# A hybrid decoder layer in five fronts: one, two, two, two and one block instead of four pairs

## The chip, the cores and the metric

The kernel runs on one core of a Trainium2 chip. The metric is device time in microseconds (us) of one execution: the median of 3 runs was 4762.22 us before the change (4757.62 to 4777.23).

## What is computed

One decoder layer for 1024 prompt tokens and 8 sample tokens, everything in fp32, D = 1024:

```python
h = RMSNorm(x)
x = x + W_out(sigmoid(gate_ssd) * SSD(h) + sigmoid(gate_rwkv) * RWKV7(h))   # one projection of h, 7952 columns
x = x + MemCrossAttn(RMSNorm(x), mem_k, mem_v)                              # 4 heads, 256 memory tokens
x = x + PEER(RMSNorm(x))                                                    # per token 8 heads x 16 experts
y = RMSNorm(x)
```

SSD and RWKV-7 carry a state from token to token, so blocks of tokens go in order. PEER chooses 128 experts a token out of 16384 (two score vectors of 128 a head, their 16 best each, the 16 best of the sums), and computes `sum_k gate_k * gelu(x . U[i_k]) * V[i_k]` with the rows of two tables of 64 MB each.

## The kernel before

The 1024 prompt tokens are 8 blocks of 128, numbered 0 to 7. `front(gi)` (L464) takes a group of blocks (`GROUPS`, L20: four pairs) through everything up to the choice of experts: the **mixer** (norm, all columns of `w_in` in 31 weight tiles of 1024 x 256, each loaded in two halves of 512 KB; convolution, SSD; the RWKV inputs, a 31-step inverse of triangular 32 x 32 blocks at L843; the gates), then `scan(b)` a block, two chunks each, then `rest` (L1036): `w_out`, `w_mq`, attention over the memory, `w_mo`, `w_pq`, scores and the choice (`Best.add`, `Best.pairs`, tiles `q3b`). Products are `by_channel` (a 128 x 128 weight piece is stationary, the tokens move) or `by_token` (the tokens are stationary, 256 weight columns move).

Front 0 computes its mixer with split numbers: `parts` (L282) writes each weight tile as a rounded fp32r part and the rest (a ScalarE copy, a VectorE subtraction at L292, 1024 columns each), `Parts` does the same with the tokens, and `three` (L295) makes three products of a pair. It uses seven row buffers (tag `U`) and `xa` buffers for that. Its `rest` runs one block at a time (`SPLIT`). `memory()` (keys and values of the memory, through two `xa` buffers and `U` rows) and `keys()` are written behind front 0's scans, `sample_recurrences` behind front 0. Fronts 1 and 2 carry the 8 sample tokens along.

Experts work on one block and one of its 128 choices at a time. `u_step` gathers a row of U for each token (an indirect DMA that POOL issues, 512 KB, into a `U` row buffer) and multiplies it with x on VectorE (L1518). `v_step` (L1554) gathers a row of V and adds it, times its coefficient, on VectorE (L1570); for the k in `slots` TensorE adds it through a diagonal matrix (tile `dg`, PSUM tile `pv`). Beside front 1 stand the U and V steps of blocks 0 and 1, beside front 2 U of 2 and 3 and V of 2, beside front 3 U of 4 and 5 (`GATHERED`, L38); behind these V of block 3 (VectorE) and of block 4 (half of its steps on TensorE, `LATE_SLOTS`). The fronts' buffers are then closed, and in their space lie a 128 KB a partition matrix `cmat` and new rows. U of block 6 follows, and then V of blocks 5 and 6 by a **dense sum** (L1625): `spread` (L1591) writes each token's coefficients into `cmat` (128 tokens x 16384), and all of V passes in 128 blocks of 128 rows (`Vx`) through TensorE. One block in three multiplies plain fp32, the others split numbers. Between the dense blocks stand U and V of block 7, with 48 V steps on TensorE (`TAIL_SLOTS`, L34).

What is ready on an engine, and not yet held back by a buffer, is put in order when the program is built: program order is the priority, and a planner interleaves the engines' queues by its own costs. In program order front gi stands ahead of the expert steps of the group before it. Buffers of one tag go round in program order. Weights are loaded by the SyncE queue, gathers by POOL's.

## Time and profile before

| | before |
|---|---|
| median of 3 runs | 4762.22 us |
| profiled execution | 4803.32 us (span of its instructions 4801.6) |
| granted TensorE clock, mean | 0.800 |
| bytes moved by DMA | 1369.20 MB, mean 285 GB/s |

Busy tenths in 40 slices of 120 us (9 is 90% or more; PEclk is the granted TensorE clock in tenths; DMA the mean busy share of the 16 DMA engines):

```profile
PE   7889865769887786687676953588867964089995
DVE  4662296998878779988786899877773798786775
PEclk9988887889856896888668976688578985589997
DMA  4342589899978997999799897999788888889997
```

How to read the rows below. A row of a window table reads: stretch in us from the span's start, its length, then for each engine its busy time and its instructions (all: PE matmul, PEld weight load, DVE = VectorE, ACT = ScalarE, POOL = GpSimd; filtered by a line or a tile: only the engines that work on it), then the granted TensorE clock, the busy share of the DMA engines, and GB/s. A row of a line or form reads: line, engine, operation, out<-in with buffer numbers left out, partitions x elements, count | busy us, mean ns of one | idle us before it and what ended it. A row of a tile reads: shortest/median/longest in ns, first to last start in us. L114 is the helper `mm`, L120 the helper `copy`, L256 `weights`, L1514 `gather`.

### The profile page before, as it was taken

The page shows a single profiled execution, that of the slowest core. Times are in us where ns is not written, and L with a number is a line of the kernel's source. Part 1 is how long each engine was busy: PE and PEld are TensorE (multiplying, and loading weights), DVE is VectorE, ACT ScalarE, POOL GpSimd, SP SyncE. Part 2 cuts the span into 40 slices and gives each one's busy share as a digit, 9 for nine tenths or more (in the row PEclk, how much of TensorE's full clock was granted, in tenths as well). Part 3 has the DMA queues.
Part 4 walks back from the last instruction along what each step waited for, and adds up shares of the span by engine and source line. Part 5 has one row for each costly group of instructions (what it writes and reads, how often), then busy time and mean ns, then how long its engine had stood idle before and what let it go on. Part 6 is the DMA issues. An engine that isn't in the chain of part 4 may idle for free.

```text
span 4801.6 us, 56531 instructions
## 1 busy us (share of the span) xinstructions
PE 3581.8 (75%) x18486; PEld 2721.1 (57%) x18486; DVE 3656.8 (76%) x7730; ACT 1345.3 (28%) x3461; POOL 2456.4 (51%) x2059
## 2 busy tenths in 40 slices
PE   7889865769887786687676953588867964089995
PEld 6778764557565674365555742465655623056663
DVE  4662296998878779988786899877773798786775
ACT  5544322123132221232232311231321222143331
POOL 0000044765657644655566567745563566754444
PEclk9988887889856896888668976688578985589997
DMA  4342589899978997999799897999788888889997
GB/s 121 99 140 62 195 285 324 269 319 347 342 256 301 360 345 255 343 331 340 269 312 337 318 322 246 335 296 331 224 314 284 283 290 272 309 285 364 354 363 266
DMA packets 609102, 1369.20 MB, mean 285 GB/s; under 512 B 86124, under 2 KB 332296, under 8 KB 608800
## 3 DMA queue, kind: packets, MB, share of 16 engines
q0 software_dynamic: 260352, 948.03, 55.8%
q1 hardware_dynamic: 348456, 417.57, 26.2%
q8 instruction: 146, 2.39, 0.2%
q14 instruction: 148, 1.21, 0.1%
HBM read 1335.60 MB, written 29.90 MB: 284 GB/s over the span
## 4 chain that ended last, share of the span: by engine, by line
PE 40%; DVE 29%; DMA 11%; issue 10%; ACT 5%; POOL 4%; SPq 1%; another core or an unknown queue 0%; POOLq 0%; DVEq 0%; ACTq 0%
PE pp L114 21%; PE pc L114 10%; DVE U L1518 8%; DVE acc L1570 4%; PE pv L114 4%; POOL U L1514 4%; DMA U<-in_expert_u_dram,idx 3%; DMA U<-in_expert_v_dram,idx 2%; PE pg L114 2%; DVE q3b L452 2%; DVE vs L1618 1%; PE tp L114 1%; DMA w<-in_w_in_dram 1%; DVE f L581 1%; DVE q3b L455 1%
## 5 line engine op out<-in xcount | busy, mean ns | idle before, releaser
L1514 POOL DMA_INDIRECT U<-in_expert_u_dram,idx x1024 | 1280.9, 1251 | 828.9 <-DVE act L1518 249.4
L1518 DVE CUSTOM_DVE_ANT_0 U<-U,xa 128x1024 f32<-128x1024 f32 x1032 | 1271.1, 1239 | 140.8 <-DMA U<-in_expert_u_dram,idx 132.8
L1514 POOL DMA_INDIRECT U<-in_expert_v_dram,idx x768 | 900.7, 1173 | 751.4 <-DVE act L1518 248.0
L1570 DVE SCALAR_TENSOR_TENSOR acc<-U,cf,acc 128x1024 f32<-128x1024 f32 x656 | 863.5, 1316 | 111.4 <-DMA U<-in_expert_v_dram,idx 102.5
L114 PE MATMUL pp<-qw,w 128*128 128x256 f32 (+2 forms) x2872 | 731.3, 407 | 159.6 <-issue 43.8
L114 PEld LDWEIGHTS pp<-qw,w 128*128 128x128 f32 x2872 | 580.6, 214 | 281.8 <-issue 107.3
L114 PE MATMUL pp<-w,qw 128*128 128x256 f32 (+1 forms) x2528 | 623.0, 400 | 116.8 <-ACT f L856 44.5
L114 PEld LDWEIGHTS pp<-w,qw 128*128 128x128 f32 (+1 forms) x2528 | 477.4, 192 | 242.7 <-ACT f L856 46.9
L114 PE MATMUL pv<-U,dg 128*128 128x512 f32 x448 | 240.8, 669 | 99.1 <-DMA U<-in_expert_v_dram,idx 85.6
L114 PEld LDWEIGHTS pv<-U,dg 128*128 128x128 f32 x448 | 88.8, 209 | 217.5 <-issue 147.6
L114 PE MATMUL pc<-vs,cs 128*128 128x512 f32 x510 | 204.3, 455 | 1.9 <-DVE vs L1648 1.9
L114 PE MATMUL pp<-q,w 128*128 128x128 f32 (+1 forms) x1024 | 187.2, 340 | 4.5 <-DMA w<-in_w_pq_dram 3.3
L123 POOL TENSOR_TENSOR q3b<-q3b,q3b 128x400 f32<-128x400 f32 (+1 forms) x130 | 152.1, 1184 | 55.8 <-DVE q3b L452 53.2
L114 PEld LDWEIGHTS pp<-q,w 128*128 128x128 f32 x1024 | 163.3, 202 | 19.1 <-issue 3.7
L114 PE MATMUL pp<-vs,cs 128*128 128x512 f32 x510 | 172.2, 392 | 0.0
L114 PE MATMUL pc<-rst,q 64*64 64x64 f32 x1024 | 170.5, 305 | 2.2 <-issue 1.2
L114 PE MATMUL pg<-q,q 64*128 64x128 f32 (+1 forms) x384 | 110.8, 447 | 71.6 <-DMA q<-kt_d 33.3
L306 PE MATMUL tp<-ident,g 128*128 128x128 f32 (+1 forms) x296 | 60.8, 340 | 138.0 <-DVE g L1020 50.5
L114 PE MATMUL pc<-g,q 128*64 128x64 f32 x1024 | 140.0, 317 | 23.1 <-issue 16.6
L1648 DVE TENSOR_TENSOR vs<-Vx,vs 128x512 fp32r<-128x512 f32 x170 | 111.7, 688 | 42.1 <-ACT vs L120 35.0
L114 PEld LDWEIGHTS pg<-q,q 64*128 64x128 f32 (+1 forms) x384 | 82.5, 276 | 94.1 <-ACT q L1130 40.1
L306 PEld LDWEIGHTS tp<-ident,g 128*128 128x128 f32 (+1 forms) x296 | 43.2, 179 | 157.7 <-issue 56.2
(506 smaller groups left out, 6336.3 us busy)
## 6 DMA issues: line engine op xcount, KB each, us to landing
w<-in_w_in_dram SPq DMA_DIRECT2D x248, 512.0 KB
Vx<-in_expert_v_dram SPq DMA_DIRECT2D x128, 512.0 KB
w<-in_w_pq_dram SPq DMA_DIRECT2D x80, 512.0 KB
w<-in_w_out_dram SPq DMA_DIRECT2D x40, 512.0 KB
w<-in_w_mq_dram SPq DMA_DIRECT2D x40, 512.0 KB
w<-in_w_mo_dram SPq DMA_DIRECT2D x40, 512.0 KB
U<-in_expert_u_dram,idx POOLq DMA_INDIRECT x1024
U<-in_expert_v_dram,idx POOLq DMA_INDIRECT x768
```

The lines of the kernel that those rows point to most:

```text
L114: T.matmul(out, a, b, start=first, stop=last)
L123: G.tensor_tensor(out, a, b, op=op)
L306: T.transpose(p[:, j * P:j * P + n], x[:, c * P:(c + 1) * P], ident[:n, :n])
L452: V.tensor_tensor(oh[:n], iota50[:n, None, :].to_broadcast([n, 8, NCAND]), posf[:n, h, k8].unsqueeze(2).to_broadcast([n, 8, NCAND]), op=OP ...
L455: V.tensor_reduce(idf[:n, h, k8], oh[:n], axis=AX.X, op=OP.add)
L581: V.scalar_tensor_tensor(acc[:, 3 - k:TP], p[:, :TP - 3 + k], cw(k), acc[:, 3 - k:TP], op0=OP.mult, op1=OP.add)
L1514: G.indirect_dma_start(out=dst, out_offset=None, in_=table, in_offset=bass.IndirectOffsetOnAxis(ap=idx, axis=0))
L1518: V.tensor_tensor_reduce(out=u, in0=u, in1=x, scale=1.0, scalar=0.0, op0=OP.mult, op1=OP.add, accum_out=out)
L1570: V.scalar_tensor_tensor(z["acc"], v, cf, z["acc"], op0=OP.mult, op1=OP.add)
L1618: V.tensor_scalar(rb[:, a, :], iota, by[:, 1, t0 + a:t0 + a + 1], by[:, 2, t0 + a:t0 + a + 1], op0=OP.is_equal, op1=OP.mult)
L1648: V.tensor_tensor(vl, v[:, s], vh.bitcast(F32), op=OP.subtract)
```

## The change

`GROUPS` becomes (0), (1, 2), (3, 4), (5, 6), (7), with `rest` once a front. Front 0 multiplies plain fp32, and the second half of its weight tiles lies in `U` rows (`wide`). Beside front 1 stand U and V of block 0, beside front 2 of blocks 1 and 2, beside front 3 of 3 and 4, all V steps on VectorE; beside front 4, block 7 alone, U of 5 and 6. Behind the last front come the first 32 U steps of block 7, `spread` of blocks 5 and 6, and their dense sum with the rest of block 7's steps between its blocks; V follows U by 32 steps, and 16 V steps are on TensorE. Dense blocks of V are now 128 successive rows instead of every 128th, and lie in the `U` rows too, of which there are nine there instead of five.

```diff
@@ -17,26 +17,21 @@
 P = 128
 D = 1024
 NS = 8
-GROUPS = ((0, 2), (2, 2), (4, 2), (6, 2))
+GROUPS = ((0, 1), (1, 2), (3, 2), (5, 2), (7, 1))
 TMAX = 256
 Z0, XBC0, DT0, RW0, GS0, GR0 = 0, 1024, 2560, 2576, 5904, 6928
 EC = math.exp(-0.5)
 NCAND = 50
 ROWS = ((0, 1, 16), (1, 1, 8), (2, 1, 5), (3, 1, 4), (4, 1, 3), (5, 3, 2), (8, 8, 1))
-NQ3, NG4, NXA, NK1, NU, NUT, NVX, NVS, NW, NAC = 26, 6, 2, 5, 7, 5, 4, 6, 5, 1
+NQ3, NG4, NXA, NK1, NU, NUT, NVS, NW, NAC = 26, 6, 2, 5, 7, 9, 6, 5, 1
 NQ3B, NSC = 5, 3
-ORDER = 0
 SATT = (0, 3)
-MPOS = 2
-SPLIT = (0,)
-AHEAD = 2
-LATE_SLOTS = ((), tuple(range(0, 16, 2)))[:AHEAD]
-TAIL_SLOTS = tuple(range(0, 16, 3))
+LEAD = 2
+TAIL_SLOTS = tuple(range(0, P, 8))
 ACT_A = range(0, 32, 2)
 SPLIT_V = 3
 PB = 16
-GATHERED = ((0, 1), (0,), ())
-PE_SLOTS = ()
+GATHERED = ((0,), (0, 1), (0, 1), ())
 
 
 def ap4(a, offset, dims):
@@ -250,11 +245,11 @@
         j = f2().bitcast(BF) if j is None else j
         S.activation(j[:n, :], x, AF.Square, accum_out=ss)
 
-    def weights(w, c0, n=256, split=False):
-        x = Weights()
+    def weights(w, c0, n=256, wide=False):
+        x = Weights(wide)
         for i in range(2):
             load(x.half[i][:, :, :n], w[i * 512:(i + 1) * 512, c0:c0 + n].rearrange("(k p) c -> p k c", p=P))
-        return parts(x) if split else x
+        return x
 
     def wtile(dt=F32):
         return t("w", [P, 4, 256], NW, dt)
@@ -262,40 +257,12 @@
     class Weights:
 
 
-        def __init__(self):
-            self.half = [wtile() for _ in range(2)]
+
+        def __init__(self, wide):
+            self.half = [wtile(), rowt().rearrange("p (k c) -> p k c", k=4) if wide else wtile()]
 
         def of(self, k, s):
             return self.half[k // 4][:, k % 4, s]
-
-    class Parts:
-
-
-        def __init__(self, n):
-            self.hi = [t("qw", [P, 2, TMAX + NS], 4, F32R) for _ in range(4)]
-            self.lo = [t(tag, [P, D], bufs, F32R)[:, :3 * n].rearrange("p (k x) -> p k x", k=3)
-                       for tag, bufs in (("U", n_u()), ("U", n_u()), ("xa", NXA))]
-
-        def of(self, k, s):
-            return self.hi[k // 2][:, k % 2, s], self.lo[k // 3][:, k % 3, s]
-
-    def parts(wt):
-
-        def row():
-            return t("U", [P, D], n_u(), F32R).rearrange("p (k x) -> p k x", k=4)
-
-        hi, lo = [], []
-        for i, w in enumerate(wt.half):
-            hi.append(row())
-            copy(hi[i], w)
-            lo.append(row() if i else wtile(F32R))
-            V.tensor_tensor(lo[i], w, hi[i].bitcast(F32), op=OP.subtract)
-        return [tuple(x[k // 4][:, k % 4, :] for x in (hi, lo)) for k in range(8)]
-
-    def three(out, a, b, first, last):
-
-        for i, (x, y) in enumerate(((a[0], b[0]), (a[0], b[1]), (a[1], b[0]))):
-            mm(out, x, y, first and i == 0, last and i == 2)
 
     def to_cols(x, n, dst, t0, wname=None):
 
...
@@ -323,17 +282,11 @@
 
     def by_channel(wt, j, h, n, p):
         for k in range(8):
-            if isinstance(h, Parts):
-                three(p[:, :n], [x[:, j * P:(j + 1) * P] for x in wt[k]], h.of(k, slice(0, n)), k == 0, k == 7)
-            else:
-                mm(p[:, :n], wt.of(k, slice(j * P, (j + 1) * P)), h[k // 2][:, k % 2, :n], k == 0, k == 7)
+            mm(p[:, :n], wt.of(k, slice(j * P, (j + 1) * P)), h[k // 2][:, k % 2, :n], k == 0, k == 7)
 
     def by_token(wt, h, t0, n, p, nw=256):
         for k in range(8):
-            if isinstance(h, Parts):
-                three(p[:n, :nw], h.of(k, slice(t0, t0 + n)), wt[k], k == 0, k == 7)
-            else:
-                mm(p[:n, :nw], h[k // 2][:, k % 2, t0:t0 + n], wt.of(k, slice(0, nw)), k == 0, k == 7)
+            mm(p[:n, :nw], h[k // 2][:, k % 2, t0:t0 + n], wt.of(k, slice(0, nw)), k == 0, k == 7)
 
     kt2_d = dr.tile([2, P, 8, P], F32, name="kt2_d")
 
...
@@ -499,7 +452,7 @@
                 next(satt)
 
         for i in range(4):
-            wt = weights(w_in, Z0 + i * 256, split=sa)
+            wt = weights(w_in, Z0 + i * 256, wide=sa)
             aside_satt(SATT[0])
             s2 = slice(i * 256, i * 256 + 256)
             for b, (t0, n) in enumerate(body):
...
@@ -1205,26 +1150,14 @@
                 res.append((row0[nl], NS) + sample_choice())
             return res
 
-        if gi in SPLIT and ORDER:
-            res = []
-            for b in range(nb):
-                scan(b)
-                if gi == 0 and b == 0 and MPOS:
-                    memory()
-                    keys()
-                res += rest([b])
-        else:
-            for b in range(nb):
-                scan(b)
-                if gi == 0 and b + 1 == MPOS:
-                    memory()
-                    keys()
-            if last and ORDER == 0:
-                final_states()
-            res = [x for b in range(nb) for x in rest([b])] if gi in SPLIT else rest(list(range(nb)))
-        if last and ORDER:
+        for b in range(nb):
+            scan(b)
+        if gi == 0:
+            memory()
+            keys()
+        if last:
             final_states()
-        return res
+        return rest(list(range(nb)))
 
 
     def b8(x, off, n):
...
@@ -1560,12 +1493,12 @@
         v = rowt()
         gather(v, V_tab, z["ix"][:, k:k + 1])
         cf = z["cf"][:, k:k + 1]
-        if k % PB in slots:
+        if k in slots:
             dg = t("dg", [P, P], 2)
             copy(dg, ident, scale=cf)
             for hf in range(2):
                 s = slice(hf * 512, (hf + 1) * 512)
-                mm(z["pv"][:, s], dg, v[:, s], k == slots[0], k == P - PB + slots[-1])
+                mm(z["pv"][:, s], dg, v[:, s], k == slots[0], k == slots[-1])
         else:
             V.scalar_tensor_tensor(z["acc"], v, cf, z["acc"], op0=OP.mult, op1=OP.add)
         if k == P - 1:
@@ -1590,15 +1523,15 @@
 
     def spread(cmat, blocks):
 
-        for b, z in blocks:
+        for b, z in enumerate(blocks):
             parts, ii = (t("vs", [P, 512], NVS) for _ in range(2))
             parts = parts[:, 0:384].rearrange("p (i k) -> p i k", i=3)
             ix = z["idx"].rearrange("p h k -> p (h k)")
             hi, lo = (ii[:, i * P:(i + 1) * P].bitcast(I32) for i in range(2))
             V.tensor_scalar(hi, ix, 7, None, op0=OP.arith_shift_right)
             V.tensor_scalar(lo, ix, P - 1, None, op0=OP.bitwise_and)
-            V.tensor_copy(parts[:, 0, :], hi)
-            V.tensor_copy(parts[:, 1, :], lo)
+            V.tensor_copy(parts[:, 0, :], lo)
+            V.tensor_copy(parts[:, 1, :], hi)
             p = tp()
             for i, x in enumerate((parts[:, 0, :], parts[:, 1, :], z["cf"])):
                 T.transpose(p[:, i * P:(i + 1) * P], x, ident)
@@ -1628,10 +1561,9 @@
         acc = []
         for b in range(len(blocks)):
             acc.append((pc(), pc()) if b % 2 == 0 else (pp(), pp()))
-        rows = V_tab.rearrange("(a c) d -> c a d", c=P)
         for c in range(P):
-            v = t("Vx", [P, D], NVX)
-            load(v, rows[c])
+            v = rowt()
+            load(v, V_tab[c * P:(c + 1) * P, :])
             if c % SPLIT_V == 0:
                 for hf in range(2):
                     for b in range(len(blocks)):
...
@@ -1733,41 +1665,29 @@
         late += [x for i, x in enumerate(z) if i not in GATHERED[gi - 1]]
         samples(chosen)
         chosen = ahead
-    for slots in LATE_SLOTS:
-        z = late.pop(0)
-        for k in range(P):
-            v_step(z, k, slots)
     fronts.close()
     rows_late = ctx.enter_context(tc.tile_pool(name="rows_late", bufs=1, reuse_waits="tile"))
-    for tag in ("U", "Vx", "cs", "by"):
+    for tag in ("U", "cs", "by"):
         pools[tag] = rows_late
     pools["wd"] = ctx.enter_context(tc.tile_pool(name="wd", bufs=1, reuse_waits="tile"))
     cmat = t("cmat", [P, P, 2 * P], 1)
-    chosen = prompts(chosen)
     z = start(chosen[0])
-    for k in range(P):
-        u_step(z, k)
-    late.append(z)
-    z = start(chosen[1])
-    late.append(z)
-    dense = late[:2]
-    for b, x in enumerate(dense):
-        spread(cmat, [(b, x)])
     steps = []
-    others = late[2:]
-    for n in range(P // PB):
+    for n in range(P // PB + LEAD):
         for k in range(n * PB, n * PB + PB):
-            steps.append((u_step, late[-1], k))
-            if others[0] is not late[-1]:
-                steps.append((v_step, others[0], k, TAIL_SLOTS))
-            elif n:
-                steps.append((v_step, late[-1], k - PB, TAIL_SLOTS))
-    rest = range(P) if others[0] is not late[-1] else range(P - PB, P)
-    steps += [(v_step, late[-1], k, TAIL_SLOTS) for k in rest]
+            if k < P:
+                steps.append((u_step, z, k))
+            if n >= LEAD:
+                steps.append((v_step, z, k - LEAD * PB, TAIL_SLOTS))
+    for step, *x in steps[:LEAD * PB]:
+        step(*x)
+    steps = steps[LEAD * PB:]
+    spread(cmat, late)
     at = 0
-    for c, _ in enumerate(dense_sum(dense, cmat)):
+    for c, _ in enumerate(dense_sum(late, cmat)):
         while at < len(steps) * (c + 1) // P:
-            steps[at][0](*steps[at][1:])
+            step, *x = steps[at]
+            step(*x)
             at += 1
 
 
```

## Rows read from the trace of the kernel before

**Rows 1.** Page: busy time by engine; the chain that ended last.

```profile
PE 3581.8 (75%) x18486; PEld 2721.1 (57%) x18486; DVE 3656.8 (76%) x7730; ACT 1345.3 (28%) x3461; POOL 2456.4 (51%) x2059
...
PE 40%; DVE 29%; DMA 11%; issue 10%; ACT 5%; POOL 4%; SPq 1%; another core or an unknown queue 0%; POOLq 0%; DVEq 0%; ACTq 0%
```

**Rows 2.** Busy time of all engines, by stage.

```profile
0.00:360.00 360.00, 296.15 (x2100) 264.62 (x2101) 218.00 (x450) 181.15 (x421) 10.93 (x51) 0.91 0.42 120
360.00:523.00 163.00, 162.85 (x1461) 135.77 (x1460) 36.70 (x69) 72.46 (x224) 9.54 (x8) 0.82 0.26 78
523.00:842.00 319.00, 212.40 (x1281) 188.70 (x1279) 216.90 (x569) 79.24 (x196) 116.49 (x80) 0.80 0.83 288
842.00:1753.00 911.00, 723.41 (x3830) 555.14 (x3830) 759.45 (x1428) 237.30 (x661) 562.66 (x455) 0.80 0.90 317
1753.00:2731.00 978.00, 722.37 (x3725) 548.38 (x3725) 822.46 (x1860) 246.55 (x670) 575.53 (x474) 0.78 0.91 317
2731.00:3937.00 1206.00, 855.18 (x3964) 624.10 (x3962) 960.37 (x2184) 272.40 (x730) 726.87 (x608) 0.77 0.84 290
3937.00:4183.00 246.00, 71.67 (x279) 57.40 (x279) 203.44 (x419) 54.35 (x130) 166.05 (x134) 0.53 0.86 292
4183.00:4802.00 619.00, 537.80 (x1856) 346.95 (x1856) 439.46 (x755) 201.84 (x433) 288.38 (x251) 0.92 0.89 324
```

**Rows 3.** Tiles in_w_in (front 1) and in_w_pq (front 0, block 0): weight loads.

```profile
L256 SPq DMA_DIRECT2D w<-in_w_in_dram x62: 166/368/1244, 842.2 to 1303.1; - x62
...
L256 SPq DMA_DIRECT2D w<-in_w_pq_dram x16: 368/387/963, 592.5 to 653.8; - x16
```

**Rows 4.** Front 0: splitting, one fp32r form (0 to 360); scan, memory, first gathers.

```profile
L292 DVE TENSOR_TENSOR w<-w,U 128x1024 fp32r<-128x1024 f32 x31 | 37.9, 1223 | 25.7 <-ACT U L120 25.7
...
L292 DVE TENSOR_TENSOR U<-w,U 128x1024 fp32r<-128x1024 f32 x31 | 37.9, 1223 | 12.6 <-PE pp L114 12.3
...
L114 PE MATMUL pp<-qw,U 128*128 128x264 f32 x456 | 110.4, 299 | 10.1 <-DVE f L581 7.6 <-DVE q L709 2.0 <-DVE st L670 0.5
...
L911 SPq DMA_DIRECT2D tx<-td x32: 302/412/1557, 356.4 to 3457.4; - x32
...
L114 PE MATMUL pv<-xa,U x128: 379/379/797, 468.1 to 524.0; 128*128 128x256 f32 x128
...
L1514 POOL DMA_INDIRECT U<-in_expert_u_dram,idx x27: 936/1031/1987, 704.1 to 799.5; - x27
```

**Rows 5.** PE by line and form: plain fp32 products.

```profile
L114 PE MATMUL pp<-w,qw 128*128 128x256 f32 x2272 | 558.1, 398 | 92.9 <-ACT f L856 31.3 <-DVE g L511 20.5 <-DVE g L1055 14.0
...
L114 PE MATMUL pp<-q,w 128*128 128x128 f32 x512 | 70.1, 297 | 4.0 <-DMA w<-in_w_pq_dram 3.3 <-ACT q L120 0.6
```

**Rows 6.** Windows of line L1518, then of line L1570.

```profile
842.00:1753.00 911.00, 261.38 (x422) 0.80 0.90 317
...
842.00:3937.00 3095.00, 953.39 (x1624) 0.78 0.88 307
...
842.00:1753.00 911.00, 277.37 (x211) 0.80 0.90 317
...
842.00:3937.00 3095.00, 745.47 (x564) 0.78 0.88 307
```

**Rows 7.** Window of tile q3b (the choice): DVE, ACT, POOL.

```profile
0.00:4802.00 4802.00, 446.80 (x2159) 35.30 (x96) 193.11 (x162) 0.80 0.82 285
```

**Rows 8.** Windows of tiles in_expert_u, then in_expert_v: POOL, the gathers issued.

```profile
842.00:2731.00 1889.00, 594.59 (x478) 0.79 0.90 317
...
842.00:2731.00 1889.00, 452.92 (x369) 0.79 0.90 317
```

**Rows 9.** Windows of the tail: second spread, dense sum, end.

```profile
4183.00:4271.00 88.00, 59.40 (x281) 47.19 (x282) 84.29 (x210) 49.82 (x121) 50.49 (x39) 0.73 0.74 234
4271.00:4710.00 439.00, 437.06 (x1490) 280.26 (x1490) 308.95 (x489) 142.79 (x293) 196.66 (x177) 1.00 0.97 361
4710.00:4802.00 92.00, 41.34 (x88) 19.50 (x86) 46.22 (x57) 9.22 (x20) 41.23 (x37) 0.71 0.68 235
```

More of the change, by code (lines that the diff above doesn't have):

```diff
@@ L308, in to_cols @@
                 src = p.rearrange("p (j t) -> p j t", j=4)[:, 2 * j2:2 * j2 + 2, :n]
-                if isinstance(dst, Parts):
-                    for j in range(2):
-                        k = hf * 4 + 2 * j2 + j
-                        hi, lo = dst.of(k, slice(t0, t0 + n))
-                        copy(hi, src[:, j], scale=col(wname, k))
-                        V.scalar_tensor_tensor(lo, src[:, j], col(wname, k), hi.bitcast(F32),
-                                               op0=OP.mult, op1=OP.subtract)
-                    continue
                 out = dst[hf * 2 + j2][:, :, t0:t0 + n]
@@ L486, in front @@
             rstd(ss[:, nb:], NS, 1, 1.0 / D, 0)
-        hT = Parts(TT_) if sa else [qw() for _ in range(4)]
+        hT = [qw() for _ in range(4)]
         for i, (t0, n) in enumerate(blocks):
@@ L521, in front @@
             for k in range(8):
-                xs = [x.bitcast(F32) for x in hT.of(k, slice(t0, t0 + n))] if sa else [hT[k // 2][:, k % 2, t0:t0 + n]]
-                for i, x in enumerate(xs):
-                    mm(p[:n, b * 16:b * 16 + 16], x, wdt[:, k, :], k == 0 and i == 0, k == 7 and i == len(xs) - 1)
+                mm(p[:n, b * 16:b * 16 + 16], hT[k // 2][:, k % 2, t0:t0 + n], wdt[:, k, :], k == 0, k == 7)
         def softplus(n, s):
@@ L564, in front @@
         for i in range(6):
-            wt = weights(w_in, XBC0 + i * 256, split=sa)
+            wt = weights(w_in, XBC0 + i * 256, wide=sa)
             aside_satt(SATT[1])
@@ L713, in front @@
         lor = q3()
-        wt = weights(w_in, RW0 + 3072, split=sa)
+        wt = weights(w_in, RW0 + 3072, wide=sa)
         mix(wt, 24, lor)
@@ L733, in front @@
             k_ = q3()
-            mix(weights(w_in, RW0 + 8 * P + q * 256, split=sa), 8 + 2 * q, k_)
+            mix(weights(w_in, RW0 + 8 * P + q * 256, wide=sa), 8 + 2 * q, k_)
             for j in range(2):
@@ L752, in front @@
             for base, dst in ((0, r_), (16, v_)):
-                mix(weights(w_in, RW0 + base * P + q * 256, split=sa), base + 2 * q, dst)
+                mix(weights(w_in, RW0 + base * P + q * 256, wide=sa), base + 2 * q, dst)
             lw, ta, kk = q3(), q3(), q3()
@@ L849, in front @@
         for i in range(4):
-            wt = weights(w_in, GS0 + i * 256, split=sa)
+            wt = weights(w_in, GS0 + i * 256, wide=sa)
             s2 = slice(i * 256, i * 256 + 256)
@@ L864, in front @@
             load(g2, I["rwkv_g2"][0, :, qs])
-            wt = weights(w_in, GR0 + q * 256, split=sa)
+            wt = weights(w_in, GR0 + q * 256, wide=sa)
             for b, (t0, n) in enumerate(body):
@@ L1100, in rest @@
             nbs = len(body)
-            if gi == 0 and bl[0] == 0 and MPOS == 3:
-                memory()
-                keys()
             kt = [q3() for _ in range(4)]
```

9 lines of the change are left out of this document (2 added, 7 removed).

## The prediction

> **What bounds the kernel now.** I read the page first, then the busy time of each engine by stage, then single lines. The page says that no engine is full over the whole span: DVE is busy 76%, PE 75%, and the chain that ended last passes through PE, DVE and DMA in turn [rows 1]. The stages say more [rows 2]. For the first 523 us the chip works on front 0 alone: the DMA engines are busy 42% and then 26%, and DVE 218 of 360 and 37 of 163 us. From 842 us on, where the gathers of expert rows run beside the fronts, DVE is busy 83% and 84% and the DMA engines 90% and 91% at 317 GB/s. So the kernel has an underused head of some 700 us and a long middle in which DVE and DMA are both nearly full. Two more stretches are looser than the middle: front 3 (2731 to 3937), whose DVE is at 80% at 290 GB/s, and 3937 to 4183, where the rows of block 6 are multiplied before the dense sum can begin. Each expert step costs DVE 261.38/211 = 1.24 us (first table) or 277.37/211 = 1.31 us (second) [rows 6] and 0.524 MB of transfer.
>
> I call A the time until front 1 begins to load its weights, B front 1, C the rest until the last front ends, D the tail. In the kernel before A ends at 842 [rows 3].
>
> **A: front 0 with one block in plain fp32.** Gone: the 62 subtractions that split weights (37.9 us for each 31, so 76 us of DVE [rows 4]), the ScalarE copies before them, and the second block. PE: 1488 fp32r records (456 of them in the row shown) stand for 496 products of three, 304 by channel and 192 by token. Of the 296 us that PE was busy in the first 360 us I give about 50 to other work, so 246 us, 0.5 us a product. After, 304 products move 136 columns and 96 move 256. Plain fp32 is two records a product: 70.1/256 = 0.274 us at 128 columns, 558.1/1136 = 0.491 us at 256 [rows 5]. That gives 304 x 0.291 + 96 x 0.491 = 136 us, with 25 us of other work 161. At PE's 82% busy share that is 196 us; with start-up I take the scan to begin at 220 (bounds: half of 356, 178; and 356 less the 76 us of splitting, 280), where it began at 356 [rows 4].
> The Trainium skill ("FP8 and Floating Point Precision", TensorE Precision Notes) says that true fp32 takes four passes through the array, so against three products it would cost a third more a column. By that rule the products would take 246 x 4/3 x (304 x 136/264 + 96)/496 = 168 us, not 136, and A some 35 us more; the rows at 128 columns are cheaper than this, and the sum goes by the rows.
> Scan and memory keys: 356 to 530 before (the last product of memory() ended at 524), with PE busy 162.85 of 163 us [rows 2, 4]. One scan of two goes; memory() stays whole, and its row buffers come free only as front 0's last weights are consumed. I take 130 us (between half of 174 and all of it), to 350. In rest() the output and query projections pass under this; attention, w_mo and w_pq follow. Before, that took from memory's end near 530 to the last w_pq load at 654 [rows 3]; I take 95 of these 124, so A ends at 445. The sample recurrences need memory's buffers; the first gather came 179 us behind memory's end (704 against 525 [rows 4]), so it now comes at about 530.
>
> **B: front 1 with the rows of one block.** Before, 911 us beside 211 steps of each table. PE was busy 723 of them [rows 2], and its work stays: that is the floor, 911 the ceiling. Now there are 128 + 128 steps from 530 on; at the old pace, 0.23 of each a us, they are used up near 1085, two thirds into the front, and nothing else is ready. I give the front two thirds of the 188 us it waited: 785 us, so B ends at 1230. DVE has about 220 + 327 us for it and is no limit; it idles 200 us here, which is the price of starting with one block.
>
> **C: fronts 2 and 3 (two blocks), front 4 (one).** Rows: U of blocks 1 to 6, V of blocks 1 to 4, 768 + 512 steps. The V steps that ran late (block 3) or half on PE (block 4, 64 steps) now all run on DVE beside the fronts. DVE by rows: the three fronts from 842 to 3937 left 759 + 822 + 960 - 953 - 745 = 843 us without expert steps, 281 a front [rows 2, 6]. Front 4 I put at 160 (the 31-step inverse and the fixed part of an instruction don't halve; bounds 140 and 281). Choosing the experts of blocks 1 and 2 falls behind front 1, so C holds seven blocks of it where its fronts' share is 5.5: 1.5 x 447/8 = 84 us [rows 7]. The products of the sample's attention stay, 32 us within the U line. Sum: 562 + 160 + 84 + 32 + 768 x 1.24 + 512 x 1.31 = 2460 us. At DVE's share from 842 to 2731, (759 + 822)/1889 = 0.837, that is 2940 us. DMA by rows: 478 + 369 gathers [rows 8] are 444 MB of the 317 x 1889 = 599 MB there, so a front brings 77 MB, and a front of one block brings the same weights: 1280 x 0.524 + 3 x 77 = 902 MB, at 317 GB/s 2845 us. I take 2890, between the two: the mix is heavier in DVE and lighter in DMA than the one whose shares I use. C ends at 4120, where the kernel before had ended its last front at 3937 and block 6's rows at 4183.
>
> **D: the tail.** Two spreads of 88 us each, the first now not beside block 6's rows but beside block 7's. In the old second spread DVE was busy 84 of 88 us and 39 rows were gathered [rows 9]; two of them give 176 us and 78 rows. Left are 384 - 78 = 306 rows of 0.524 MB (with V's dense blocks), at the 361 GB/s of the dense stretch 444 us. There PE was busy 437 of 439 us; it loses 32 of 48 V steps, so it is no longer the limit, and DVE (309 of 439) takes their 42 us. With 20 us for the last norm: 640 us (600 to 680; it was 619 with one spread). The row buffers (nine for all, where five served gathers and four the dense rows) and the contiguous dense blocks I cost at nothing: the stretch was at 97% DMA share [rows 9]; ends -20 and +20.
>
> Sum 445 + 785 + 2890 + 640 = 4760 us. The profiled execution took 4803.3 with a span of 4801.6, so 4762; the median of the runs is 4762.2/4803.3 = 0.9914 of it: **4721 us**, 0.9% faster. 0.5%, 24 us, is about what a measurement can tell from no change: below 4738 is faster, above 4786 slower.
>
> **Rivals.** (1) *Front 1 does not go faster without rows* (slower). Its 911 us would then be set by its own chain, not by rows taking DVE, and A's gain is lost in it, since only one block's rows are ready. For it: PE busy 723, and the scan's chain doesn't shorten. Against it: the mixers grow from front to front with the U steps beside them. Price 126 us: 4888, on the median's scale 4846. The sign turns at a B of about 835 us.
> (2) *DVE's share of the whole doesn't rise* (slower). DVE work grows: 3657 - 76 + 96 x 1.31 (V steps off PE) + 36 (two single fronts for one double) = 3743. From 842 to the end DVE was busy 3185 of 3960, 80.4% [rows 2]; with some 190 us of DVE done by 445, 3553/0.804 + 445 = 4864, so 4823. For it: fuller stretches are short; against it: the two loosest, 2731 to 4183, go.
> (3) *The middle fills better* (faster). Both V streams beside each front give DVE something ready throughout. At 0.88, C is 2795 us and the time 4667, 4627 on the median. Against: the rest stages are held by DMA.
> (4) *Front 0 ends later than 445*: memory() waits until the scan is done, or fp32 is dearer than the rows say. With all 174 us behind the scan, A is 490 to 500 and the time near 4775: no change that counts.
>
> **Chances.** Forecast 0.45 (own range 4660 to 4780: faster 0.30, same 0.13, slower 0.02); (1) 0.20 (slower 0.19, same 0.01); (2) 0.12, slower; (3) 0.13, faster; (4) 0.10 (0.02, 0.05, 0.03). Together faster 0.45, same 0.19, slower 0.36. The range, 4600 to 4860, reaches from (3) to (1).
>
> **What would show it.** The scan of front 0 begins near 220, front 1's first w_in load is near 445 and the first gather near 530 (right for A); front 1's loads to front 2's first are 785 us apart, with no gather in the last 150 us (B; 911 would mean rival 1); the last front's pairs end near 4120 with U of block 6 done by then (C); the dense stretch has PE below 95% and the tail is 640 us (D). The forecast is wrong if C's DVE share stays under 0.82 or B exceeds 835 us.

## The result, and the profile after: 2.4% slower

The changed kernel takes 4880.61 us (median of 4 runs, 4877.43 to 4882.78) against 4762.04 (4757.62 to 4777.23): 1.0239 times as long, 95% interval [1.0214, 1.0264]. The forecast was 4721, its range 4600 to 4860. The profiled execution after lies on its median (4880.9, span 4879.2); the one before that the forecast was made from lay 41 us above its own.

The page after: busy time by engine, then busy tenths in 40 slices of 122 us.

```profile
PE 3469.7 (71%) x18230; PEld 2690.8 (55%) x18230; DVE 3727.3 (76%) x8003; ACT 1291.2 (26%) x3472; POOL 2545.9 (52%) x2067
...
PE   7897669788786797867846878576257553069998
...
DVE  3415998972189989786999988669987758897887
...
PEclk9888779867896898578967985787578566579999
DMA  6547699971468899799978998998899898857998
```

TensorE lost 112 us of work and VectorE gained 70 [rows 1]. The slices show the trouble at once: in the ninth to the eleventh, near 980 to 1340 us, DVE falls to 7, 2, 1 and the DMA engines to 7, 1, 4. The kernel before had no stretch in its middle in which both fell together. The stages after, as windows (the columns as in [rows 2]); they are front 0 until its scan, front 0's rest, front 1's mixer, front 1's scan and rest, fronts 2, 3 and 4, the rows of block 6 that were left, and the tail:

```profile
0.00:227.00 227.00, 183.81 (x1188) 157.92 (x1189) 97.49 (x329) 98.74 (x323) 12.64 (x53) 0.92 0.61 184
227.00:473.00 246.00, 207.59 (x1481) 178.48 (x1477) 71.21 (x175) 80.58 (x216) 17.11 (x11) 0.88 0.58 190
473.00:1000.00 527.00, 391.88 (x1728) 289.49 (x1727) 484.30 (x937) 115.07 (x298) 349.21 (x257) 0.83 0.87 303
1000.00:1382.00 382.00, 324.12 (x2096) 261.80 (x2096) 137.16 (x359) 117.79 (x358) 58.57 (x44) 0.76 0.40 133
1382.00:2355.00 973.00, 735.17 (x3743) 552.39 (x3741) 823.60 (x1749) 236.75 (x660) 590.20 (x483) 0.79 0.91 320
2355.00:3313.00 958.00, 678.65 (x3578) 546.28 (x3576) 820.74 (x1698) 241.33 (x651) 582.43 (x488) 0.78 0.90 311
3313.00:4130.00 817.00, 425.40 (x2440) 354.71 (x2439) 662.29 (x1609) 165.03 (x445) 511.39 (x397) 0.68 0.89 308
4130.00:4260.00 130.00, 0.00 (x0) 0.00 (x0) 110.14 (x216) 2.40 (x6) 104.20 (x86) 0.50 0.88 307
4260.00:4879.00 619.00, 523.11 (x1991) 349.69 (x1991) 520.40 (x940) 233.53 (x518) 320.18 (x254) 0.93 0.86 330
```

The ends of these stages are read from rows of tiles: front 1's and front 2's loads of `w_in`, the gathers of block 0's rows of U and V, and the first load of front 0's scan (`tx`).

```profile
L251 SPq DMA_DIRECT2D w<-in_w_in_dram x62: 367/368/1843, 473.0 to 982.1; - x62
...
L251 SPq DMA_DIRECT2D w<-in_w_in_dram x62: 367/368/5062, 1381.9 to 1900.9; - x62
...
L1447 POOL DMA_INDIRECT U<-in_expert_u_dram,idx x128: 935/1226/8980, 541.1 to 1042.7; - x128
...
L1447 POOL DMA_INDIRECT U<-in_expert_v_dram,idx x128: 936/1014/3036, 595.5 to 1077.5; - x128
...
L859 SPq DMA_DIRECT2D tx<-td x32: 302/410/4096, 227.1 to 3814.3; - x32
```

| step | forecast | after | difference |
|---|---|---|---|
| A, to front 1's first load | 445 | 473 | +28 |
| B, front 1 | 785 | 909 | +124 |
| C, to the first spread | 2890 | 2878 | -12 |
| D, tail | 640 | 621 | -19 |
| sum, on the scale of profiled executions | 4760 | 4881 | +121 |

The other 39 us between 4721 and 4881 are the factor 0.9914, by which the sum was carried from that one execution to the median. What the changed kernel gained up to front 1 (842 to 473 us) it needs again behind it: front 1 takes what it took before, 909 against 911 [rows 2], with 256 row steps beside it instead of 422 (211 on each table [rows 6]).

### The profile page after: what moved, and what is told of

Same layout as the page of the kernel before. It is cut to its first block, busy times and chain, and to the rows that moved or that the text cites. A ratio compares the mean times of both kernels' runs of the same rounds, so it can differ in the third digit from the quotient of the medians.

```text
span 4879.2 us, 56374 instructions
## 1 busy us (share of the span) xinstructions
PE 3469.7 (71%) x18230; PEld 2690.8 (55%) x18230; DVE 3727.3 (76%) x8003; ACT 1291.2 (26%) x3472; POOL 2545.9 (52%) x2067
## 5 line engine op out<-in xcount | busy, mean ns | idle before, releaser
L1447 POOL DMA_INDIRECT U<-in_expert_u_dram,idx x1024 | 1326.3, 1295 | 862.1 <-DVE acc L1503 250.2
L1451 DVE CUSTOM_DVE_ANT_0 U<-U,xa 128x1024 f32<-128x1024 f32 x1032 | 1289.2, 1254 | 200.0 <-DMA U<-in_expert_u_dram,idx 196.8
L1447 POOL DMA_INDIRECT U<-in_expert_v_dram,idx x768 | 945.4, 1231 | 601.1 <-DVE act L1451 208.5
L109 PE MATMUL pp<-qw,w 128*128 128x256 f32 (+3 forms) x3632 | 850.7, 397 | 309.3 <-issue 103.5
L1503 DVE SCALAR_TENSOR_TENSOR acc<-U,cf,acc 128x1024 f32<-128x1024 f32 x752 | 989.0, 1315 | 68.9 <-DMA U<-in_expert_v_dram,idx 63.0
L109 PEld LDWEIGHTS pp<-qw,w 128*128 128x128 f32 x3632 | 698.8, 223 | 445.6 <-issue 245.0
L109 PE MATMUL pp<-w,qw 128*128 128x256 f32 (+1 forms) x2720 | 683.2, 411 | 146.9 <-ACT f L807 49.3
L109 PEld LDWEIGHTS pp<-w,qw 128*128 128x128 f32 (+1 forms) x2720 | 524.7, 197 | 289.3 <-ACT f L807 53.2
L109 PE MATMUL tp<-vs,vs 128*128 128x128 f32 x256 | 45.3, 324 | 177.2 <-DVE vs L1551 177.2
L109 PEld LDWEIGHTS pc<-vs,cs 128*128 128x128 f32 x510 | 94.1, 188 | 88.1 <-ACT vs L115 38.0
L109 PEld LDWEIGHTS tp<-vs,vs 128*128 128x128 f32 x256 | 39.0, 226 | 183.4 <-ACT vs L1545 155.1
```

The source lines that it names most:

```text
L109: T.matmul(out, a, b, start=first, stop=last)
L1447: G.indirect_dma_start(out=dst, out_offset=None, in_=table, in_offset=bass.IndirectOffsetOnAxis(ap=idx, axis=0))
L1451: V.tensor_tensor_reduce(out=u, in0=u, in1=x, scale=1.0, scalar=0.0, op0=OP.mult, op1=OP.add, accum_out=out)
L1503: V.scalar_tensor_tensor(z["acc"], v, cf, z["acc"], op0=OP.mult, op1=OP.add)
```

## The experiments

The theory behind the first runs: row steps delay front 1 only in its mixer, and the hole behind it, with nothing to gather, is lost. Its rivals: the front's own chain sets its time (rival 1), or the work of VectorE as a whole does (rival 2).

**Front 1 with no rows, and with twice the rows** (one run each). The first leaves out block 0's experts (its output is without them); the second works through them twice.

```diff
 # e1
+        if gi == 1:
+            acc = t("acc", [P, D], NAC)
+            load(acc, x2_d[r0:r0 + P, :])
+            finish(acc, P, O["y_prompt"][0, r0:r0 + P, :])
+            z = []
...
 # e2
+        for _ in range(2 if gi == 1 else 1):
+            z = experts(prompts(chosen), GATHERED[gi - 1])
```

> The changed kernel without the 128 U and 128 V steps of block 0 (block 0's expert sum is left out). Theory 1, front 1 is set by its own chain once its rows are used up: of front 1's 909 us (its first w_in load at 473 to front 2's first at 1382) only the mixer gets shorter, from 527 to about 400 us (PE was busy 392 in it); scan and rest stay at 196 + 186, so front 1 takes 780 to 830 us and the whole 4750 to 4800. Rival, expert rows cost the same wherever they stand and the loss is the fifth front's work: the 256 rows have 327 us of DVE in them, and at 0.84 busy the whole falls by 390, to about 4490.

> The changed kernel with block 0's expert steps done twice (256 rows more, 134 MB, 327 us of DVE). Theory 1: the stretch 1080 to 1382 of front 1 has 226 us of idle DVE and a DMA share of 0.30, so most of the added rows fit in it: the whole grows by 80 to 170 us, to 4960 to 5050. Rival: rows cost the same everywhere, 327/0.84 = 390 us more, about 5270.

4721.85 us, just below the theory's range, and 5093.39, between the theory's and the rival's. Front 1's mixer, and its scan and rest, without rows:

```profile
467.00:818.00 351.00, 307.53 (x1563) 237.11 (x1563) 231.53 (x585) 101.87 (x277) 48.57 (x35) 0.94 0.39 119
818.00:1227.00 409.00, 355.06 (x2270) 279.00 (x2271) 90.14 (x318) 121.27 (x366) 9.43 (x9) 0.81 0.26 83
```

and with twice the rows:

```profile
472.00:986.00 514.00, 389.52 (x1725) 288.44 (x1724) 470.35 (x923) 112.99 (x295) 338.84 (x249) 0.84 0.86 303
986.00:1421.00 435.00, 337.94 (x2114) 269.63 (x2113) 324.42 (x578) 129.15 (x374) 270.27 (x211) 0.73 0.88 314
```

Without rows the front takes 760 us, with one block's 909, with twice these 949. So rival 1 is wrong in its reason: the front does go faster without rows. But the first 256 steps cost it 149 us and the next 256 only 40, and the mixer is as long with one block's rows (527) as with two (514). It is filled to the same level either way: VectorE is busy 484 of 527 and 470 of 514 us, and 232 of 351 without rows. The kernel before shows the same, once its front 1 is cut in two where the mixer ends:

```profile
842.00:1326.00 484.00, 384.46 (x1737) 285.18 (x1737) 441.60 (x872) 108.96 (x289) 307.33 (x249) 0.87 0.92 320
1326.00:1753.00 427.00, 338.95 (x2095) 269.96 (x2093) 317.85 (x556) 128.34 (x372) 255.33 (x206) 0.72 0.88 314
```

In the mixer VectorE was busy 91%, in scan and rest 74%. The DMA engines were fuller there too (0.87 in the mixer with rows, 0.39 without), but they are not what the mixer waited for: of the 135 us that TensorE stood idle in it with one block's rows, 73 ended on VectorE, 30 on ScalarE and 1 on a transfer (without rows 24 of 37 on VectorE, none on a transfer). Two things beside these waits are in the 176 us between 351 and 527. The granted clock was 0.83 with the rows and 0.94 without, and the same 608 records of one form took 435 ns instead of 395. And the cut is one by time: without rows 165 records fewer (1563 instead of 1728) lie before it. The doubled rows weren't free: fronts 2 and 3 took 996 and 990 us where they take 973 and 958, and the run ends 213 us later.

**Two blocks first, the single ones last.** If the hole were the price, a front 0 of two blocks, which leaves no hole, would win it back.

```diff
-GROUPS = ((0, 1), (1, 2), (3, 2), (5, 2), (7, 1))
+GROUPS = ((0, 2), (2, 2), (4, 2), (6, 1), (7, 1))
-GATHERED = ((0,), (0, 1), (0, 1), ())
+GATHERED = ((0, 1), (0, 1), (0,), ())
```

> The changed kernel with groups of 2, 2, 2, 1, 1 blocks (five fronts and plain fp32 as before, but front 1 has the rows of two blocks beside it; dense blocks 5 and 6). Theory 1: front 0 ends near 710 instead of 473, front 1 again takes some 910 but carries 512 rows, and the empty stretch is gone: 4770 to 4830, faster than the change. Rival (the price is that of five fronts): 4870 to 4890, as the change.

4873.46 us, 1.0222 [1.0185, 1.0259]: the rival's number. The hole is gone, and the end moves by 7 us, which is within the two intervals. So there is a second price, in the five fronts themselves.

**The small edits of the tail, and of the V steps.** Three runs: the kernel before with successive rows in the dense blocks; the changed one with 96 more V steps on TensorE (64 of block 4, and 48 of block 7 instead of 16); the changed one with V of block 7 four groups behind U instead of two.

```diff
 # e4, on the kernel before
-            load(v, rows[c])
+            load(v, V_tab[c * P:(c + 1) * P, :])
 # e5, on the changed one
+        z = experts(..., tuple(range(0, P, 2)) if gi == 3 else ())   # block 4
-TAIL_SLOTS = tuple(range(0, P, 8))
+TAIL_SLOTS = tuple(k for k in range(P) if k % 16 % 3 == 0)
 # e8, on the changed one
-LEAD = 2
+LEAD = 4
```

> The kernel before with the dense sum's blocks of V as 128 successive rows instead of every 128th row (and the two halves of the index exchanged for it), nothing else. The dense stretch of the changed kernel ran at 383 GB/s where that of before ran at 361. If successive rows are the cause: 439 us shrink to about 415 and the whole to 4735 to 4745. If the nine shared row buffers are the cause: no change, 4755 to 4770.

> The changed kernel with as many V steps on TensorE as the kernel before: every second one of block 4 (64) and 48 of block 7, so 96 steps of 1.31 us, 126 us, less on DVE. Theory 2, DVE's work sets the time (DVE busy 3727 in the change, 3657 before, idle 1152 and 1145 us): the time falls by half to all of the 126 us, to 4760 to 4820. Theory 1 (the empty stretch of front 1 alone is the loss): DVE in the middle has slack behind DMA, the time stays within 25 us, 4855 to 4890.

> The changed kernel with 64 instead of 32 U steps of block 7 ahead of the two spreads, and V 64 steps behind U. In the trace of the change the DMA share is 0.08 from 4355 to 4407 us, because the next rows stand behind dense blocks in the shared row buffers and those wait for the second spread. If that hole is a loss: 25 to 45 us less, 4835 to 4855. If rows only move from one place to another in a tail set by other work: 4870 to 4890.

The first gives 4767.28, 0.9991 [0.9971, 1.001]: nothing, as costed in the prediction. The second gives 4880.22, 1.024 [1.0218, 1.0262]: VectorE works 116 us less (3611) and the end doesn't move, so VectorE's work by itself is not what the end follows. The 64 steps of block 4 did bring the spread forward, by 31 us (4229); the tail, with its 32 added V steps on TensorE, took that back: 651 us, PE busy 571 where it was 523. The third gives 4906.36, 1.031 [1.0285, 1.0335], above both expectations. It was meant to fill the 52 us in which only the second spread ran, with the DMA engines at 8% (second row below, of the changed kernel: first spread, second, dense stretch, end); it only made the spreads longer, 178 us against 147.

```profile
4260.00:4355.00 95.00, 56.52 (x264) 45.15 (x265) 93.13 (x234) 48.89 (x120) 56.83 (x43) 0.69 0.82 288
4355.00:4407.00 52.00, 38.62 (x269) 34.47 (x269) 46.52 (x149) 46.49 (x118) 0.95 (x1) 0.93 0.08 26
4407.00:4790.00 383.00, 355.35 (x1207) 222.50 (x1208) 313.94 (x474) 113.89 (x234) 226.62 (x180) 1.00 0.99 383
4790.00:4879.00 89.00, 72.62 (x255) 47.56 (x253) 66.81 (x84) 24.26 (x48) 35.79 (x30) 0.90 0.81 323
```

**V of both blocks beside each front, in the kernel before.**

```diff
-AHEAD = 2
+AHEAD = 0
-GATHERED = ((0, 1), (0,), ())
+GATHERED = ((0, 1), (0, 1), (0,))
```

> The kernel before with V of blocks 3 and 4 beside the fronts as their U steps go (all on VectorE) instead of late, half of block 4 on TensorE: two constants. It is the order of expert steps of the change without its fifth front. If an even mix of U and V beside each front is worth something (the prediction's rival 3): 4690 to 4740. Theory 2 (84 us more of DVE work): 4790 to 4830.

4735.40 us, 0.994 [0.9922, 0.9958], in the first range and not in that of the theory of VectorE's work: VectorE works 65 us more (3722) and the time falls. This part of the change is a gain.

**Plain fp32, alone and undone.** First the changed kernel with front 0's numbers split as before; then the kernel before with plain fp32 in its two-block front 0, and nothing else.

```diff
 # e7, on the changed one
-            wt = weights(w_in, Z0 + i * 256, wide=sa)
+            wt = weights(w_in, Z0 + i * 256, split=sa)
 # e11, on the kernel before
-            wt = weights(w_in, Z0 + i * 256, split=sa)
+            wt = weights(w_in, Z0 + i * 256, wide=sa)
 ...
```

> The five fronts, expert order and tail of the change, with front 0 in split numbers as before. If plain fp32 in the first front is what made the change slower: 4800 to 4850. By the prediction's step A (plain fp32 costs a single block nothing: the scan began at 227 us): no gain, the 76 us of subtractions come back, 4880 to 4920.

> The kernel before, with only its front 0 (still two blocks) in plain fp32 as in the changed kernel. Splitting 31 weight tiles took 122 us to the end of a one-block front 0. Theory (a front 0 of two blocks is bound by its products, and front 1's mixer by VectorE, so that an earlier start of front 1 only brings its rows into the mixer): scan at 315 to 325 where it was 356, front 1's mixer ends within 20 us of 1326, time 4735 to 4775. Rival (what front 0 gains goes to the end one to one, as with one block): 36 us or more of front 0 and the 76 us of VectorE, 4660 to 4725.

5002.87, 1.049 [1.0456, 1.0523], which is 122 us more than the changed kernel, and its scan begins at 349 instead of 227, the same 122 us: with one block, what front 0 gains goes to the end whole. Both expectations were too low, that by the prediction's step A by 83 us. With two blocks plain fp32 gives 4738.25, 0.996 [0.9936, 0.9985]: the scan begins at 324 instead of 356, front 1's mixer ends at 1292 instead of 1326, and 22 us come to the end, inside the theory's range for the time, though its mixer moved by 34 us where the theory allowed 20.

**The rows held back from the mixer.** If VectorE is full only in the mixer, block 0's steps should stand beside scan and rest. A zero taken from a tile of front 1 is added to the x that they multiply. First it comes from the last gate of the mixer, then from the second quarter of the RWKV inputs, near its middle.

```diff
+        if r0 == 0:
+            V.tensor_scalar(x, x, held["x"][:, 0:1], None, op0=OP.add)
 # in front 1; e9: gg[0][1][:, 511:512], behind the gates; e10: kk[:, 0, 0:1] for q == 1
+            V.tensor_scalar(held["x"], kk[:, 0, 0:1], 0.0, None, op0=OP.mult)
```

> The changed kernel, but the x of block 0's experts waits for the last gate of front 1's mixer (one added value a partition, zero), so that its 256 row steps are worked on beside front 1's scan and rest instead of beside its mixer. So far the mixer took 527 us with the rows (VectorE busy 484) and 351 without (VectorE busy 232), scan and rest 382 and 409. Theory (VectorE is the bound of the mixer alone, and rows delay the front only there): mixer 350 to 370, scan and rest 420 to 445 as with the doubled rows (435), front 1 790 us, front 2's first load near 1265, the time 4740 to 4800. Rival (work is only moved: the rows delay whatever stands beside them): front 1 again 880 to 920, time 4860 to 4900. Third way (rows are left over and paid later): front 1 near 790, but the end moves by less than 60 us, 4820 to 4860.

> The same wait, but for a value of the second of four quarters of front 1's RWKV inputs, near the middle of its mixer, so that about a third of the row steps can stand beside the rest of the mixer. Theory: mixer 410 to 440, scan and rest 390 to 420, front 1 near 820, time 4770 to 4820, between the changed kernel and the longer wait. If the longer wait leaves rows over that are paid later, this one is the faster of the two, 4740 to 4790. Rival (work is only moved): 4860 to 4900.

4858.36, 1.0204 [1.0184, 1.0224], and 4812.17, 1.0126 [1.0095, 1.0157]. Mixer (to the first load of the scan, as in the rows above), then scan and rest, with the longer wait:

```profile
469.00:823.00 354.00, 305.62 (x1538) 235.82 (x1536) 231.84 (x582) 96.58 (x268) 58.97 (x42) 0.94 0.41 127
823.00:1306.00 483.00, 382.03 (x2288) 298.57 (x2289) 345.34 (x612) 134.31 (x385) 282.37 (x225) 0.75 0.84 299
```

and with the shorter one:

```profile
467.00:910.00 443.00, 366.35 (x1716) 272.48 (x1716) 347.63 (x755) 106.50 (x288) 183.25 (x134) 0.89 0.63 217
910.00:1326.00 416.00, 332.88 (x2110) 266.62 (x2109) 282.58 (x544) 125.05 (x366) 219.09 (x167) 0.75 0.77 274
```

The same steps, moved by one wait, and front 1 takes 837 and 859 us instead of 909. So the place of the rows, with their number unchanged, made 50 to 72 of the 124 us that B was over. The longer wait helps the front more and the end less (22 us against 68). What the traces show beside this is that by it block 0's last gathers come behind front 2's first load (1306), by the shorter one at 1215, 110 us ahead of that load (1326); that this is the reason is not shown. The times are those of the third way for the one (rows left over) and of the theory for the other; the front itself got longer than either said, 837 for 790 and 859 for 820. With the longer wait the mixer is as short as the theory had it (354 us, that without rows 351), and scan and rest are longer (483 us, said 420 to 445): there the rows delay the front too. The 256 steps cost it 77 us when they are held back (837 against 760), and 149 when they are not.

**What the fifth front costs.** The two gains of the change together, on four fronts (plain fp32 in front 0, V beside each front): the twin of the run with two blocks first. Then the same with the wait of the middle. Last the changed kernel with one tile of `w_in` loaded in front 4 and used 31 times (block 7's values are then not the reference's).

```diff
 # e14
+        if once and w is w_in:          # in the last front
+            return once[0]
```

> The kernel before with plain fp32 in its front 0 and with both blocks' V steps beside each front: four fronts, and otherwise as the five fronts of two, two, two, one and one block, which took 4873. So this run prices the fifth front with its tail alone. Alone the two edits gave 25 and 22 us. Theory (the two are in different stages, front 0 and fronts 1 to 3, and add): 4700 to 4725, and the fifth front costs 150 to 170 us. Rival (both only fill the same slack of VectorE, and the second gives nothing): 4728 to 4745, fifth front 130 to 145.

> The four fronts of the run beside it, with the x of block 0's experts waiting for the second quarter of front 1's RWKV inputs, as in the five fronts, where that took 68 us off. Theory (the mixer of front 1 is bound by VectorE, and its rows are better placed later wherever there is room): front 1's mixer shorter by 50 us or more, but here its 512 row steps need some 660 us of VectorE beside a scan and rest of 430 us, so that rows are left over: between 30 us faster and 10 us slower than without the wait. Rival (the wait only idles VectorE, and the middle is bound by the sum of its row steps): slower by 20 to 60 us.

> The changed kernel, whose front 4 loads one tile of w_in and uses it for all 31 (so block 7's values are not the reference's): 30 loads of 1 MB less, its instructions unchanged. Of the middle the last thing to end is U of block 6 (4250), 120 us behind front 4's own end, with the DMA engines at 0.88 to 0.89. Theory (the fifth front costs its transfers, which take the gathers' room): 31 MB at 308 GB/s are 102 us; time 4775 to 4825. Rival (VectorE's row steps or the front's chain of work set that end): 4850 to 4885.

4709.90 us, 0.9884 [0.9855, 0.9912]: the two gains add, and this is faster than either kernel. Against five fronts, 4873, the price of the fifth front, with all that came with it (the order and the row buffers of the tail, `rest` of front 0 in one piece), is 163 us. The traces place it: 34 us lie ahead of the last fronts (2734 against 2700), where both kernels work on the same six blocks, 120 in the last fronts and 7 in the tail. In the twin, the last front with the rows behind it to its second spread, and the tail:

```profile
2700.00:4084.00 1384.00, 777.86 (x3969) 617.00 (x3968) 1210.28 (x2704) 309.75 (x800) 890.17 (x731) 0.70 0.87 301
4084.00:4705.00 621.00, 541.02 (x1857) 348.52 (x1857) 440.07 (x755) 203.80 (x435) 297.49 (x252) 0.91 0.88 324
```

With two blocks first, the two single fronts to the first spread, and the tail:

```profile
2734.00:4238.00 1504.00, 799.30 (x4762) 671.34 (x4761) 1203.75 (x2819) 304.32 (x873) 920.98 (x735) 0.70 0.90 315
4238.00:4866.00 628.00, 524.89 (x1991) 350.06 (x1991) 521.17 (x940) 233.70 (x518) 320.44 (x255) 0.93 0.85 325
```

VectorE did the same work, 1204 and 1210 us, in 120 us more. The DMA engines moved 474 MB instead of 417, but that explains little: without 31 MB of front 4's loads the time is 4860.82, 1.0217 [1.0186, 1.0248], 20 us less (the two intervals overlap) where the theory said 55 to 105. In that run's stretch from front 4's first load to the spread both have room, the DMA engines at 0.83 and VectorE at 0.82, and it takes 924 us instead of 947:

```profile
3305.00:4229.00 924.00, 419.18 (x2435) 350.22 (x2434) 755.88 (x1823) 167.00 (x450) 628.16 (x481) 0.66 0.83 281
```

The wait of the middle, 68 us of gain above, costs 182 us with four fronts: 4891.65, 1.0277 [1.0247, 1.0308]. The rows stop for the start of front 1 (first row), front 1 does take 844 us instead of 912, and the fronts end earlier; but then the rows are left to run without a front beside them (second row, from the last load of `w_pq` at 3602 to the second spread, 662 us; in the twin 430, from 3654). Neither expectation had a loss of that size.

```profile
784.00:1018.00 234.00, 219.27 (x1076) 172.19 (x1075) 129.16 (x384) 72.48 (x203) 20.57 (x23) 0.94 0.37 105
...
3602.00:4264.00 662.00, 106.79 (x416) 77.04 (x414) 574.53 (x1268) 75.34 (x168) 485.22 (x394) 0.54 0.85 295
```

## Why the prediction was wrong

**The ledger.** By runs in order: from 4762 plain fp32 takes 24 us (4738), V beside the fronts another 28 (4710), the fifth front with its tail adds 163 (4873), and one block first instead of two adds 7 (4881), no more than the measurements' scatter. The first two steps are one edit each; the third is the groups, the tail and its buffers at once. The forecast had the first gain, the second only as rival 3, and neither cost at its size.

**A was nearly right.** The scan began at 227 (forecast 220). The terms of plain fp32 held: the form below is one of two records a product, and 45.5 + 44.4 us are 0.296 us a product at 136 columns (forecast 0.291).

```profile
L109 PE MATMUL pp<-qw,w 128*128 128x136 f32 x304 | 45.5, 294 | 4.8 <-DVE f L532 2.5 <-DVE q L660 1.5 <-DVE f L534 0.5
L109 PE MATMUL pp<-qw,U 128*128 128x136 f32 x304 | 44.4, 289 | 0.0
```

The estimate from the Trainium skill's four passes for true fp32 ("FP8 and Floating Point Precision", TensorE Precision Notes) would have put the scan near 255. The scan at 227 doesn't bear that estimate out, which took each of a split product's three records at one pass; whether that or the four passes is off here, no run separates. Scan and memory took the 130 us of the forecast (227 to 357), the rest 116 us instead of 95. That the first gather came at 541 (530) was right too.

**B is the step that failed**, and in it two sentences: "I give the front two thirds of the 188 us it waited: 785 us", and that VectorE "has about 220 + 327 us for it and is no limit". The floor was fair (723; the run without rows has 760).

The first sentence has the share the wrong way round. Rows that last two thirds into the front should leave two thirds of the wait, so the prediction's own premise gives 723 + 125 = 848 us, and 4823 for the whole, 4783 on the median's scale: no gain. Half of B's 124 us is this slip.

The second has the size of a term wrong, and the place. VectorE worked 621 us in front 1: 328 on rows as forecast, and 294 on the rest, not 220. The sample's recurrences had ended before front 1 in the kernel before; with the shorter head, 46 us of them fell into front 1's mixer, and some 17 us more of choosing experts fell into front 1. One row of these recurrences, in the kernel before and after:

```profile
L1404 DVE TENSOR_REDUCE srsa<-U x4: 1199/1203/1205, 666.1 to 706.4; 128x16 f32<-128x1024 f32 x4
...
L1337 DVE TENSOR_REDUCE srsa<-U x4: 1200/1201/1204, 509.0 to 546.0; 128x16 f32<-128x1024 f32 x4
```

And the rows were spread evenly over the front in the sum, where in fact they are worked on as soon as they are ready. Of the 328 us of row steps in front 1, 274 were worked on in the mixer:

```profile
473.00:1000.00 527.00, 146.28 (x232) 0.83 0.87 303
...
473.00:1000.00 527.00, 127.64 (x100) 0.83 0.87 303
```

(VectorE time of L1451, then of L1503, in the mixer.) The kernel before had 287 us of rows in its mixer, nearly as many, beside 155 us of other work; now it was 210. So with half the blocks' rows the mixer got 43 us longer (484 to 527), and that ate what scan and rest gained by having few rows (427 to 382). VectorE was busy 484 of 527 us in the mixer and 137 of 382 in scan and rest. I had read front 1 as one stage of 911 us at 83% [rows 2]; cut in two it was 91% and 74%, and the first half's answer to fewer rows was there to be read. The runs with the wait show that the place counts: the same rows placed later give 50 to 72 us of B's 124 back. How the rest divides between the added work and the place, no run separates.

**Rival 1 came near in its number** (4888 on the profile's scale, 4846 on the median's, 4881 measured) and not in its reason: the front alone goes 149 us faster. That the sum met it is luck: A was 28 us over, C and D 31 under. Rival 2's number (4864, on the median's scale 4823) is near as well: VectorE's share from front 1 on, (3727 - 169)/(4879 - 473) = 0.808, did not rise over the 0.804 before. But C alone had the forecast's share, 2417 of 2878 us, 0.840; the share was lost in B, 621 of 909.

**C and D held, and the comparison behind them did not.** C's sum was right within 12 us, with 2417 us of VectorE work against 2460; the last front's pairs ended near 4130 as said, but U of block 6 was not done by then: it took 130 us more, in which TensorE did nothing. D was 621 against 640: the dense stretch went at 383 GB/s instead of 361 [rows 9], with PE at 93%. What I did not ask is whether the same two blocks cost less as one front than as two. The twin says so: 120 us in these fronts, of 163. I had priced the fifth front by its VectorE work (160 us against 281) and its bytes (77 MB), and added both; the runs show that taking work (96 V steps, 116 us) or bytes (31 MB) away again gives 0 and 20 us at the end. What else makes two single fronts longer than a double one is not settled: each takes some 740 to 820 us with PE busy 400 to 425, where a double one takes 910 to 1020 with 680 to 740.

## What to carry to other kernels

Before a cover is halved, cut the stage it covers into its own stages and read each engine's share in each: an average of 83% was 91% and 74%, and the rows, ready first, went to the fuller half. Ask too what else a shorter cover pushes into the stage behind it. Where background work was scarce, holding it back from the full half gained 68 us; where it was plentiful, the same wait cost 182. And check the share of a wait against its premise: rows that last for two thirds of a stage leave two thirds of an evenly spread wait, not one third. A pipeline stage that handles half the work is not half as long, so a stage more must be priced by a run against its twin with one less, and each good part of a mixed change deserves to be run alone: two of them together made a kernel 1.2% faster than the one before.

## What the chip showed that was not expected

A product of split numbers did not get cheaper with half the columns. With one block in front 0 (136 columns, split as before) the rows of one form, and the window to the scan, are:

```profile
L115 PE MATMUL pp<-qw,U 128*128 128x136 f32 x456 | 150.6, 391 | 1.0 <-DVE q L710 1.0
```

```profile
0.00:349.00 349.00, 298.40 (x1676) 275.49 (x1676) 173.54 (x409) 157.38 (x383) 13.60 (x53) 0.67 0.42 120
```

391 ns a record at a granted clock of 0.67, where the kernel before had 299 ns at 264 columns [rows 4] and a granted clock of 0.91 [rows 2]; the changed kernel, in plain fp32 at 136 columns, had 0.92 (all three are means between the two levels, 1.2 and 2.4 GHz, with PE busy 81 to 86% of the stretch). The same form in two stretches of the run with 136 columns, the first at the upper level and the second at the lower:

```profile
L115 PE MATMUL pp<-qw,U 128*128 128x136 f32 x54 | 12.5, 285 | 0.0
125.00:145.00 20.00, 20.00 (x172) 19.16 (x170) 12.93 (x21) 10.86 (x33) 0.00 (x0) 0.99 0.26 69
...
L115 PE MATMUL pp<-qw,U 128*128 128x136 f32 x153 | 55.3, 419 | 0.0
180.00:270.00 90.00, 86.49 (x408) 81.48 (x408) 37.90 (x101) 34.10 (x96) 0.00 (x0) 0.50 0.31 87
```

At the upper level a record took 285 ns with 136 columns and, in the kernel before (150 to 210 us, clock 1.00), 289 ns with 264: half the columns hardly shortened the record. At the lower level it took 419. From these rows an estimate of the price: a mean of 391 between 285 and 419 puts some four in five of the 912 records of 136 columns at the lower level, and there a record of any form came every 0.212 us (86.49/408) instead of every 0.116 (20.00/172), which makes some 70 of the 122 us that splitting cost the one-block front a price of the clock. Why it was lower with narrow split products, no run here shows.
